# A decoder block's way from its last dense product to its first expert: rewritten, with spare products in it, and the next down weights issued inside the first expert's branch

## The chip, the cores and the metric

The kernel runs on one core of a Trainium2 chip. The metric is device microseconds (us) of one launch; the median of the runs counts. TensorE (PE) does matrix products, PEld are its weight loads, VectorE is DVE, ScalarE is ACT, GpSimd is POOL, and SyncE (SP) issues most transfers.

## The reference, cut to what matters

The block mixes 256 tokens of 2048 channels with two recurrent mixers, projects the mix with `w_out`, and normalises. A router then picks one of 4 groups and 2 of its 8 experts for each token, and each expert's rows go through a gated layer of width 512. All is float32.

```python
x = LN(ALPHA * x + mix @ w_out)                  # 2048 x 2048: the last dense product
lg = x @ w_rg + b_rg                             # 4 groups, top 1
le = x @ w_re + b_re                             # 32 experts, top 2 in the group
for each expert e:                               # 32 experts, rows sorted by expert
    h = silu(xb @ w_gate[e]) * (xb @ w_up[e])    # 2048 -> 512, twice
    out += weight * (h @ w_down[e])              # 512 -> 2048
x = LN(ALPHA * x + out + sigmoid(x @ w_pg) * (p @ w_ple))
```

## The kernel before

The program order is written by hand, engine by engine. The first stage is dense: weights of 512 KB arrive through four staging buffers, ACT and DVE split each into a high and a low part (L217, L218, buffers in `B[6]`, `B[7]`), and PE multiplies (L282, L283, and L290 to L292 in `run`). The last four dense units are `w_out`, 512 output channels each, 16 steps `k` each. In a step PE does three products for each of the two token blocks `tb`. When a unit is done, `evac_out` adds the residual (L916), takes statistics (L932), transposes the rows (L925, copied by L927) and adds to the router's products (`logits`, L906). After the last unit come the normalisation's scale (L1117 to L1123), a second small set of products that puts the router's sums into rows (L1127), and the router itself: a chain of some 25 small DVE operations from L1201 to L1222, products that count and rank the tokens of each expert (`prk`, L1225 to L1229), and the ranks (L1238). A one-hot matrix for the first expert (`hot_quad`, L1343) lets PE pick the expert's rows (`pick`, L1414); they are transposed and scaled (`turn`, L1423 to L1428).

The second stage goes through the experts. An expert's gate and up weights are four quarters of 2 MB (`("gu", e, q)`, order `QS = (2, 1, 0, 3)`), its down weights two halves of 2 MB (`("dn", e, q)`). They live in big buffers B0 to B10; `idle` is the list of free ones, `seq` the order of the weights, and `fetch` gives the next weights of `seq` to the free buffers, on SP's queue. Five of the first ten transfers are placed between the dense weights (`HOOK_W`, numbers of loads counted from the first of `w_out`), the other five follow the last dense product. The residual rows `xres` lie in B9 until then.

For expert `e`, `up_part` multiplies the quarters (L1355, 32 products each), `glu` applies the gate (L1360 to L1362), and an expert that may have more than 32 rows has a branch on its count `c`: with more, a second set of rows is done; otherwise (`Else`) PE picks the next expert's rows (L1414) and transposes the hidden rows (L1366). Then the quarters' buffers are released and refilled, `turn` and the down products follow (`down`, L1376). For expert 0 one of the four buffers becomes the accumulator `acc` (zeroed by POOL, L1685), and the experts are sorted by count after `turn` (`sort`, L1298 to L1310); only then can SP load the weights of experts 2 and later, since their numbers come from the sort.

A wait on PE is a wait on a count that PE's instructions raise. In the program before, the count is raised once, by 64, after the fourth quarter of expert 0. What the other side of the branch would have raised is added by the first product inside `Else`. The buffers' release counts include that, so SP's first two loads after the branch and POOL's zeroing wait for that product.

## Time and profile before

| | |
|---|---|
| three runs | 1820.55 us median, 1819.59 to 1824.2 |
| the profiled execution | 1823.52 us, of them a span of 1821.8 in the profile |
| PE, DVE, ACT busy | 1599.6 us (88%), 794.0 (44%), 607.4 (33%) |
| moved by DMA | 541.38 MB, 297 GB/s over the span |
| experts' transfers on SP | 62 up, 62 gate and 60 down of 2048.0 KB, 4 down of 1024.0 KB, 10 of `w_pg` |

A busy share is an average over two different stages, so the rows to read are those by time: the 40 slices of the span, tables over chosen stretches, and the list of instructions in order of time. A row of that list gives start, duration, engine, line, operation, output from inputs, the count, and in brackets the idle time before it and what ended it. `SPq` rows are issues of transfers; `DMA_DIRECT2D` on L967 is a quarter, on L971 a down half.

### The profile page before, as it was taken

What the parts mean: (1) busy time and instruction counts of PE and PEld (TensorE: products, weight loads), DVE (VectorE), ACT (ScalarE), POOL (GpSimd) and SP (SyncE); (2) the same over time, 40 slices, a digit from 0 to 9 for tenths busy, and PEclk for the clock granted to TensorE, in tenths of its full rate; (3) what the DMA queues carried; (4) which work ended last, traced back from release to release, by engine and by line L of the source; (5) the groups of instructions that cost most, each with busy time, mean ns of one, the idle gap of its engine ahead of it and who ended that gap; (6) DMA issues with size and microseconds to landing.
All of it is one profiled execution on the core that took longest, in us unless ns stands there. A gap on an engine that the chain in (4) does not pass through costs nothing. (4 is left out here: it accounts for less than half of the span.)

```text
span 1821.8 us, 34784 instructions
## 1 busy us (share of the span) xinstructions
PE 1599.6 (88%) x14339; PEld 1081.0 (59%) x14339; DVE 794.0 (44%) x1664; ACT 607.4 (33%) x1179; POOL 26.6 (1%) x38
## 2 busy tenths in 40 slices
PE   7999999999989999997879787897797878987876
PEld 6787787877868778875447444455364433433332
DVE  5675756757765777854331121220211313221206
ACT  5645645646455465544111111111111111111122
POOL 0000000000000000000000000000000000000002
PEclk9999999999999999998899998899899998998888
DMA  7443434434336347975899999999999999999997
GB/s 243 157 153 116 157 129 134 151 117 141 127 105 196 106 139 240 362 228 222 353 426 427 426 425 426 393 425 426 426 426 426 426 426 396 385 427 425 426 426 323
DMA packets 68073, 541.38 MB, mean 297 GB/s; under 512 B 7740, under 2 KB 12108, under 8 KB 42016
## 3 DMA queue, kind: packets, MB, share of 16 engines
q1 hardware_dynamic: 67152, 537.33, 74.4%
q8 instruction: 142, 2.33, 0.5%
q0 software_dynamic: 720, 1.25, 0.3%
q14 instruction: 59, 0.48, 0.1%
HBM read 536.44 MB, written 2.36 MB: 296 GB/s over the span
## 5 line engine op out<-in xcount | busy, mean ns | idle before, releaser
L282 PE MATMUL dps<-B,B 128*128 128x512 f32 x1456 | 538.7, 410 | 12.1 <-ACT B L217 9.3
L283 PE MATMUL dps<-B,B 128*128 128x256 f32 x1456 | 411.0, 282 | 4.8 <-DVE B L218 4.7
L218 DVE TENSOR_TENSOR B<-B,B 128x512 fp32r<-128x512 f32 (+1 forms) x464 | 312.3, 683 | 188.9 <-ACT B L217 184.0
L1355 PE MATMUL dps<-B,B 128*32 128x256 f32 x3968 | 260.6, 418 | 87.9 <-DMA B<-in_w_gate_dram 39.9
L217 ACT ACTIVATE B<-B 128x512 fp32r<-128x512 f32 (+1 forms) x464 | 283.7, 623 | 161.8 <-PE dps L282 62.5
L282 PEld LDWEIGHTS dps<-B,B 128*128 128x128 f32 x1456 | 275.6, 189 | 84.5 <-ACT B L217 11.7
L283 PEld LDWEIGHTS dps<-B,B 128*128 128x128 f32 x1456 | 277.0, 190 | 12.3 <-DVE B L218 10.0
L1355 PEld LDWEIGHTS dps<-B,B 128*32 128x32 f32 x3968 | 139.3, 119 | 214.3 <-DMA B<-in_w_gate_dram 50.8
L1361 DVE SCALAR_TENSOR_TENSOR M<-M,dps 128x128 f32<-128x128 f32 x31 | 8.9, 289 | 401.9 <-ACT M L1360 401.9
L1719 ACT ACTIVATE B<-mps 32x512 f32<-32x512 f32 x120 | 70.6, 588 | 191.4 <-PE mps L1376 190.3
L1376 PE MATMUL mps<-B,M 128*32 128x512 f32 x992 | 127.4, 653 | 5.9 <-issue 2.7
L1170 PE MATMUL mps<-B,B 128*128 128x206 f32 (+1 forms) x640 | 112.8, 337 | 0.6 <-DVE B L1159 0.3
L1360 ACT ACTIVATE M<-dps 128x128 f32<-128x128 f32 x31 | 8.6, 278 | 309.1 <-PE dps L1355 309.1
L1170 PEld LDWEIGHTS mps<-B,B 128*128 128x128 f32 x640 | 110.6, 190 | 1.6 <-DVE B L1159 0.6
L1376 PEld LDWEIGHTS mps<-B,M 128*32 128x32 f32 x992 | 31.5, 118 | 83.5 <-issue 76.9
L290 PE MATMUL dps<-B,B 128*128 128x512 f32 x192 | 76.1, 396 | 2.7 <-ACT B L217 2.7
L292 PE MATMUL dps<-B,B 128*128 128x512 f32 x192 | 75.3, 392 | 0.9 <-DVE B L218 0.8
L291 PE MATMUL dps<-B,B 128*128 128x512 f32 x192 | 74.9, 390 | 0.0
L1427 DVE TENSOR_TENSOR B<-mps,V 128x512 f32<-128x512 f32 x31 | 21.4, 692 | 90.8 <-PE mps L1423 90.8
L1396 PE MATMUL mps<-B 128*128 128x512 f32 (+1 forms) x128 | 56.7, 595 | 0.7 <-ACT B L1719 0.7
L1183 DVE SCALAR_TENSOR_TENSOR C<-C,mps 128x412 f32<-128x412 f32 (+1 forms) x10 | 5.8, 581 | 102.6 <-PE mps L1175 102.6
L1182 ACT ACTIVATE C<-mps 128x412 f32<-128x412 f32 (+1 forms) x10 | 5.1, 512 | 129.9 <-issue 70.4
(465 smaller groups left out, 1585.0 us busy)
## 6 DMA issues: line engine op xcount, KB each, us to landing
B<-in_w_up_dram SPq DMA_DIRECT2D x62, 2048.0 KB, 24.5
B<-in_w_gate_dram SPq DMA_DIRECT2D x62, 2048.0 KB, 21.8
B<-in_w_down_dram SPq DMA_DIRECT2D x60, 2048.0 KB, 22.9
B<-in_w_gt_dram SPq DMA_DIRECT2D x64, 512.0 KB, 3.7
B<-in_w_rkv_dram SPq DMA_DIRECT2D x48, 512.0 KB, 3.9
B<-in_w_pg_dram SPq DMA_DIRECT2D x10, 1854.0 KB, 30.3
B<-in_w_out_dram SPq DMA_DIRECT2D x32, 512.0 KB, 3.7
B<-in_w_qk_dram SPq DMA_DIRECT2D x16, 512.0 KB, 4.0
```

The lines of the kernel that those rows point to most:

```text
L217: act.activation(h, src, AF.Copy)
L218: dve.tensor_tensor(wl[i % 4][:, :w], src, h.bitcast(FT), op=OP.subtract)
L282: mm(pt_[:, c], h[:, w], x.rearrange("p a t -> p (a t)"), start=k == 0, stop=False)
L283: mm(pt_[:, c, :256], l[:, w], x[:, 0], start=False, stop=k == nk - 1)
L290: mm(o, mh[:, ts_], h, start=first, stop=False)
L291: mm(o, ml[:, ts_], h, start=False, stop=False)
L292: mm(o, mh[:, ts_], l, start=False, stop=last)
L1170: mm(pp[:, tb], x1T[0][:, k, tb * 128:tb * 128 + 128], w[:, k, :n], start=k == 0 and tb == 0, stop=k == 15 and tb == 1)
L1355: mm(pu[32 * j:32 * j + 32].rearrange("p (a f) -> p a f", a=2), xs[:, 4 * q + k, :], w[:, :, k, 128 * j:128 * j + 128], start=q == QS[0] a ...
L1376: mm(pd[32 * j:32 * j + 32, :], hT_[:, 32 * c:32 * c + 32], w[:, c % 2, 512 * j:512 * j + 512], start=c == 0, stop=c == 3)
L1396: mm(pz, SWT[p0:p1, tb * 128:tb * 128 + 128], yq[p0:p1, o], start=True, stop=True)
L1719: act.activation(yq[32 * i:32 * i + 32, 512 * j:512 * j + 512], pd[32 * j:32 * j + 32, :], AF.Copy)
```

## The change

It has seven parts. (1) One more weight transfer is placed between the dense weights (six instead of five); the residual is loaded straight into `x1`, so that B9 is free for it. (2) In the last four steps of the last dense unit the products of token block 1 are held back, and a new `close` does them beside the first block's residual, transposes and router products. (3) The router's sums of the first three units are put into rows during the last unit (`so_far`), and the last unit's share is added in rows directly (`rest_of`). (4) Sixteen products of constants, whose result nobody reads, stand between the router's products and the rank products. (5) The rank products are four instead of five, and the first one-hot matrices are computed ahead of the counts. (6) The sort's products move into expert 0's up stage. (7) SP takes part in expert 0's branch, and on both sides of it issues expert 1's two down halves into the buffers of expert 0's first two quarters.

```diff
@@ constants
+SPARE = 16
...
-HOOK_W = (-10, -5, 1, 7, 17)
+HOOK_W = (-15, -10, -5, 1, 7, 17)
@@ run(), products of an "N" unit
+                block(0)
+                if u == len(units) - 1 and k >= 12:
+                    later.append(block)
+                else:
+                    block(1)
+            if last and later:
+                empty(100, True)
+                close(pt_, later)
+            elif last:
...
@@ logits of units 0 to 2; then, new
+    def so_far():
+
+        cmb = _carve(rw, 612, 512)
+        act.activation(cmb, held[0], AF.Copy)
+        plg.append(bank2())
+        for tb in range(2):
+            for i, (o, n) in enumerate(((0, 32), (32, 4))):
+                mm(plg[0][:, tb, o:o + n], cmb[:, 256 * i + 128 * tb:256 * i + 128 * tb + 128],
+                   cst_("eye32", n, 32 - n), start=i == 0, stop=False)
+
+    def close(p_, blocks):
+
+        x1, = xa
+
+        def turn_rows(tb):
+            pz = held[1 + tb]
+            for j in range(4):
+                pe.transpose(pz[:, j * 128:j * 128 + 128], x1[:, tb, (12 + j) * 128:(12 + j) * 128 + 128], ident)
+            act.activation(xrT[:, 12:, tb * 128:tb * 128 + 128], pz.rearrange("p (k t) -> p k t", k=4), AF.Copy)
+
+        def rest_of(tb):
+            for k in range(12, 16):
+                mm(plg[0][:, tb, :36], xrT[:, k, tb * 128:tb * 128 + 128], wrt[:, k, :], start=False, stop=k == 15)
+
+        def stats_of(tb):
+            dve.bn_stats(stats[:, tb, 3], x1[:, tb, 1536:])
+
+        add_rows(3, 0, p_)
+        act.activation(sm[:, 14:15], one_c, AF.Sqrt)
+        for b in blocks[:3]:
+            b(1)
+        turn_rows(0)
+        stats_of(0)
+        blocks[3](1)
+        add_rows(3, 1, p_)
+        rest_of(0)
+        turn_rows(1)
+        stats_of(1)
+        rest_of(1)
...
@@ where the expert weights go
-    idle, at = deque((0, 1, 2, 3, 10, 5, 9, 6, 7, 4)), {}
+    idle, at = deque((9, 0, 1, 2, 3, 10, 6, 5, 7, 4)), {}
...
-    xres = _carve(big(9), 0, 2, 2048)
-    xa.extend((x1, xres))
+    xa.append(x1)
     for tb in range(2):
-        sp.dma_start(xres[:, tb], xp[tb * 128:tb * 128 + 128, :])
+        sp.dma_start(x1[:, tb], xp[tb * 128:tb * 128 + 128, :])
...
@@ router
+    spare = bank()
+    for i in range(SPARE):
+        mm(spare[:, :128], ident, cst_("ones"), start=True, stop=True)
     prk = bank()
...
-    mm(prk[:, :32], cst_("tris"), fe(msel, 0), start=True, stop=True)
-    mm(prk[:, 32:64], cst_("ones"), fe(msel, 0), start=True, stop=False)
-    mm(prk[:, 32:64], cst_("tris"), fe(msel, 1), start=False, stop=True)
+    mm(prk[:, :64], cst_("tris"), msel.rearrange("p s g e -> p (s g e)"), start=True, stop=False)
+    mm(prk[:, 32:64], cst_("ones"), fe(msel, 0), start=False, stop=True)
...
+    hot0 = _carve(M, 0, 2, 128).rearrange("p s (e n) -> p s e n", e=4)
+    for e in range(2):
+        dve.tensor_tensor(hot0[:, :, 2 + e], rnk.rearrange("p s g e -> p s (g e)")[:, :, e:e + 1].to_broadcast([128, 2, 32]),
+                          cst_("io32", 32)[:, None, :].to_broadcast([128, 2, 32]), op=OP.is_equal)
 
     cnt, most = sb.tile([1, 32], I32, name="cnt"), V[0:1, 129:130].bitcast(I32)
...
@@ experts
-    hot_quad(0)
+    def next_down():
+
+        for key, n in early.items():
+            load(key, n)
+
+    early = {("dn", 1, i): at["gu", 0, q] for i, q in enumerate(QS[:2])}
...
-            c = count(e, engines=CE)
+            c = count(e, engines=CE if e else CE + (ENG.SP,))
...
             up_part(e, q, xg[e % 2], pu[:, 0, :256])
+            if e == 0 and q == QS[2]:
+                sort_rows()
+        if e == 0:
+            sort()
         glu(pu[:, 0, :256], hb)
...
                 turn_h(hbo[0])
+                if e == 0:
+                    next_down()
             with few.Else():
+                if e == 0:
+                    next_down()
                 first(nxt, pz)
...
-        release(*(("gu", e, q) for q in QS))
+        release(*(("gu", e, q) for q in (QS if e else QS[2:])))
...
         if e == 0:
+            at.update(early)
...
-        if e:
-            fetch()
+        fetch()
 
         turn(yo_, xg[(e + 1) % 2])
-        if e == 0:
-            sort()
-            fetch()
```

Line numbers of the changed program are higher: its dense products are L291 to L293, `close` has L941 and L946, the spare products are L1267, the rank products L1270 to L1273, `up_part` L1406, `pick` L1465, its quarter loads L1017 and down loads L1021. In the rows below `dps` and `mps` are accumulators, `B_..` big buffers, `R` and `sm` small ones, `C` the constants; an engine's name in brackets is one it waits for.

PE, end of the last dense unit, before: the last step's products, the residual's transposes and the router's products.

```order
L292 MATMUL dps<-B_70,B_6745 128x512 [waits DVE_49]
L290 MATMUL dps<-B_70,B_6745 128x512
L291 MATMUL dps<-B_70,B_6746 128x512
L292 MATMUL dps<-B_70,B_6745 128x512
L925 MATMUL mps<-C,B_7100 128x128 [waits DVE_49]
L925 MATMUL mps<-C,B_7100 128x128
L925 MATMUL mps<-C,B_7100 128x128 [waits DVE_49]
L925 MATMUL mps<-C,B_7100 128x128 x5
L906 MATMUL mps<-B_74,R 32x256 [waits Activation_49]
```

PE, the same place in the changed program, from the last step of the first block to the held-back products of the second:

```order
L291 MATMUL dps<-B_70,B_6747 128x512 [waits Activation_49]
L292 MATMUL dps<-B_70,B_6748 128x512
L293 MATMUL dps<-B_70,B_6747 128x512 [waits DVE_49]
L291 MATMUL dps<-B_70,B_6747 128x512 [waits DVE_49]
L292 MATMUL dps<-B_70,B_6748 128x512
```

and from the end of the third held-back step to the spare products:

```order
L293 MATMUL dps<-B_70,B_6747 128x512
L941 MATMUL mps<-C,B_7102 128x128 x4
L291 MATMUL dps<-B_70,B_6747 128x512
L292 MATMUL dps<-B_70,B_6748 128x512
L293 MATMUL dps<-B_70,B_6747 128x512
L946 MATMUL dps<-R,B_74 128x36 [waits Activation_49]
L946 MATMUL dps<-R,B_74 128x36 x3
L941 MATMUL mps<-C,B_7102 128x128 [waits DVE_49]
L941 MATMUL mps<-C,B_7102 128x128 x3
L946 MATMUL dps<-R,B_74 128x36 [waits Activation_49]
L946 MATMUL dps<-R,B_74 128x36 x3
L1267 MATMUL mps<-C 128x128 [waits PE_49]
```

Three steps of held-back products, one transposing of the first block, and the fourth step now stand between the two blocks' residuals; the first of the held-back products waits for DVE.

SP, from the last load that follows the dense stage, before: `B_7755` is the tenth buffer; the two loads on L971 are expert 1's down halves, L1658 and L1723 are the branch of expert 0 and what follows, L967 is the third load.

```order
L967 DMA B_7755<-in_w_up_dram 128x4096 [waits DMASW1_49,Pool_49]
L1658 UNCONDITIONAL_BRANCH
L971 DMA B_6725<-in_w_down_dram 128x4096 [waits PE_49]
L971 DMA B_6850<-in_w_down_dram 128x4096 [waits PE_49]
L1723 UNCONDITIONAL_BRANCH
L1498 TENSOR_LOAD cnt [waits DVE_49]
L1502 TENSOR_LOAD sm
L988 COMPARE_AND_BRANCH
L967 ISA
L967 DMA B_7001<-in_w_up_dram 128x4096 [waits PE_49]
```

SP, the same place in the changed program, with `L1719` the branch:

```order
L1017 DMA B_7760<-in_w_up_dram 128x4096 [waits DMASW1_49,Pool_49]
L1549 TENSOR_LOAD cnt [waits DVE_49]
L1719 COMPARE_AND_BRANCH
L1729 COMPARE_AND_BRANCH
L1729 UNCONDITIONAL_BRANCH x2
L1021 DMA B_6605<-in_w_down_dram 128x4096 [waits PE_49]
L1021 DMA B_6727<-in_w_down_dram 128x4096 [waits PE_49]
L1719 UNCONDITIONAL_BRANCH
L1021 DMA B_6605<-in_w_down_dram 128x4096 [waits PE_49]
L1021 DMA B_6727<-in_w_down_dram 128x4096 [waits PE_49]
L1719 UNCONDITIONAL_BRANCH
L1549 TENSOR_LOAD cnt [waits DVE_49]
```

The two down loads stand once on each side of the branch, with SP reading the count first. In the built program PE's count is raised by 16 after each quarter of expert 0, and the two loads wait for the counts after the first and the second quarter, which are reached before the branch; the third load (L1017, later in the order) still waits for the product inside `Else` and for the sorted counts.

More of the change, by code (lines that the diff above doesn't have):

```diff
@@ L221, in split @@
             state["split"] += 1
-    mixers, evacs = [], []
+    mixers, evacs, later = [], [], []
     clock = {"wait": 0}
@@ L286, in run, with block @@
                 mh, ml = x[:, 0], x[:, 1]
-                for tb in range(2):
-                    o = pt_[:, tb, :]
-                    ts_ = slice(tb * 128, tb * 128 + 128)
+                def block(tb, mh=mh, ml=ml, h=h, l=l, first=first, last=last, o=pt_):
+                    o, ts_ = o[:, tb, :], slice(tb * 128, tb * 128 + 128)
                     mm(o, mh[:, ts_], h, start=first, stop=False)
@@ L292, in run @@
                     mm(o, mh[:, ts_], l, start=False, stop=last)
-            if last:
+                block(0)
[7 more added lines that the diff above has]
+            elif last:
                 empty(100, True)
@@ L897, in hybrid_block @@
     lnc = _carve(V, _VEC["b_gate"], 2, 16)
-    held = []
+    held, plg = [], []
     def logits(u):
@@ L906, in logits, with add_rows @@
                 mm(held[0][32 * j:32 * j + 32, 256 * i:256 * i + 256], wrt[:, k, 4 * i:4 * i + 32], xrT[:, k, :],
-                   start=u == 0 and i == 0, stop=u == 3 and i == 1)
+                   start=u == 0 and i == 0, stop=u == 2 and i == 1)
+    def add_rows(u, tb, p_):
+        x1, = xa
+        o = slice(512 * u, 512 * u + 512)
+        dve.scalar_tensor_tensor(x1[:, tb, o], x1[:, tb, o], ALPHA, p_[:, tb], op0=OP.mult, op1=OP.add)
+    def so_far():
[7 more added lines that the diff above has]
+    def close(p_, blocks):
+        x1, = xa
+        def turn_rows(tb):
[20 more added lines that the diff above has]
+        rest_of(1)
     def evac_out(u):
         def f(p_):
-            x1, xres = xa
+            x1, = xa
             if u == 0:
@@ L914, in f @@
             for tb in range(2):
-                o = slice(512 * u, 512 * u + 512)
-                dve.scalar_tensor_tensor(x1[:, tb, o], xres[:, tb, o], ALPHA, p_[:, tb], op0=OP.mult,
-                                         op1=OP.add)
-                if u < 3:
-                    dve.bn_stats(stats[:, tb, u], x1[:, tb, o])
+                add_rows(u, tb, p_)
+                dve.bn_stats(stats[:, tb, u], x1[:, tb, 512 * u:512 * u + 512])
                 yield
@@ L928, in f @@
                 yield
-            if u == 3:
-                act.activation(sm[:, 14:15], one_c, AF.Sqrt)
-                for tb in range(2):
-                    dve.bn_stats(stats[:, tb, u], x1[:, tb, o])
             logits(u)
             yield
+            if u == 2:
+                so_far()
         return f
@@ L1114, in hybrid_block @@
     lgt = _carve(M, 0, 2, 36)
-    cmb = _carve(rw, 612, 512)
     for tb in range(2):
@@ L1118, in hybrid_block @@
     act.activation(mv[:, :, 1:2], mv[:, :, 1:2], AF.Sqrt, bias=eps_l)
-    act.activation(cmb, held[0], AF.Copy)
     dve.reciprocal(mv[:, :, 1:2], mv[:, :, 1:2])
@@ L1123, in hybrid_block @@
         dve.scalar_tensor_tensor(lgt[:, tb], wsum, nmu[:, tb], brt, op0=OP.mult, op1=OP.add)
-    plg = bank()
     for tb in range(2):
-        for i, (o, n) in enumerate(((0, 32), (32, 4))):
-            mm(plg[:, 36 * tb + o:36 * tb + o + n], cmb[:, 256 * i + 128 * tb:256 * i + 128 * tb + 128],
-               cst_("eye32", n, 32 - n), start=True, stop=True)
-    for tb in range(2):
-        dve.scalar_tensor_tensor(lgt[:, tb], plg[:, 36 * tb:36 * tb + 36], mv[:, tb, 1:2], lgt[:, tb], op0=OP.mult,
+        dve.scalar_tensor_tensor(lgt[:, tb], plg[0][:, tb, :36], mv[:, tb, 1:2], lgt[:, tb], op0=OP.mult,
                                  op1=OP.add)
@@ L1292, in ranks, with sort_rows @@
         diagonal(ec, cst_("io32", 32))
-    def sort():
+    def sort_rows():
         pz = bank()
@@ L1299, in sort @@
         act.activation(turned, pz[:32, :], AF.Copy)
+    def sort():
         po = bank()
@@ L1630, in rare @@
                 del at[key]
-    hot_quad(0)
+    def next_down():
+        for key, n in early.items():
+            load(key, n)
+    early = {("dn", 1, i): at["gu", 0, q] for i, q in enumerate(QS[:2])}
+    assert list(early) == seq[len(at):len(at) + 2]
     yo = first(0)
```

## The prediction

> **What bounds the kernel.** I read the 40 slices first.
>
> ```profile
> DMA  7443434434336347975899999999999999999997
> GB/s 243 157 153 116 157 129 134 151 117 141 127 105 196 106 139 240 362 228 222 353 426 427 426 425 426 393 425 426 426 426 426 426 426 396 385 427 425 426 426 323
> ```
>
> From the 21st slice the DMA engines are full at 425 to 427 GB/s nearly to the end, but for three slices of 385 to 396: the expert stage is bounded by its bytes. In the slices before they are not, since the free buffers and PE's pace hold them back. So the question is when the transfers become continuous. Tables over short stretches show it (PE, PEld, DVE, ACT, POOL, then granted clock, DMA share, GB/s):
>
> ```profile
> 846.00:848.00 2.00, 1.32 (x8) 0.84 (x8) 2.00 (x4) 0.49 (x2) 0.00 (x0) 1.00 0.89 205
> 870.00:872.00 2.00, 2.00 (x24) 0.96 (x20) 1.73 (x11) 0.00 (x0) 0.00 (x0) 0.50 0.77 324
> 872.00:874.00 2.00, 2.00 (x40) 1.12 (x36) 1.60 (x9) 0.00 (x0) 0.00 (x0) 0.95 0.00 0
> 878.00:880.00 2.00, 1.45 (x15) 0.74 (x8) 0.00 (x0) 0.77 (x2) 2.00 (x1) 1.00 0.78 164
> 878.50:1138.00 259.50, 213.98 (x1965) 131.60 (x1961) 54.34 (x138) 35.89 (x75) 2.85 (x1) 0.93 1.01 424
> ```
>
> Transfers run from about 847 to 871.8, stop, and resume at about 878.55 (164 GB/s in 878 to 880 is 0.77 us of full rate spread over two). The list by time of SP's issues says why:
>
> ```profile
> 845.46 1.87 SPq L967 DMA_DIRECT2D B<-in_w_up_dram  x2
> 847.51 0.84 SPq L967 DMA_DIRECT2D B<-in_w_gate_dram  x2
> 848.45 0.39 SPq L967 DMA_DIRECT2D B<-in_w_up_dram  x1
> 877.73 0.81 SPq L971 DMA_DIRECT2D B<-in_w_down_dram  x2
> 884.17 0.35 SPq L967 DMA_DIRECT2D B<-in_w_up_dram  x1
> 887.85 1.07 SPq L967 DMA_DIRECT2D B<-in_w_gate_dram  x2
> ```
>
> All ten free buffers are filled by five transfers after the dense stage; then SP waits for the first buffer that expert 0 gives back, until 877.73. Everything loaded later is the same in both programs, so the end moves with this resumption, unless a later gap opens or the transfers ahead of it are late.
>
> **The chain to that release.** Rows in order of time, from the last dense product to expert 0's end:
>
> ```profile
> 840.69 0.69 DVE L218 TENSOR_TENSOR B<-B,B 128x512 fp32r<-128x512 f32 x1 [0.67 <-ACT B L217]
> 845.26 0.39 PE L292 MATMUL dps<-B,B 128*128 128x512 f32 x1
> 845.69 1.28 DVE L916 SCALAR_TENSOR_TENSOR B<-B,dps 128x512 f32<-128x512 f32 x2 [4.31 <-PE dps L292]
> 846.43 0.44 PE L925 MATMUL mps<-C,B 128*128 128x128 f32 x2 [0.78 <-DVE B L916]
> 847.50 1.09 ACT L927 ACTIVATE B<-mps 128x512 f32<-128x512 f32 x2 [6.85 <-PE mps L925]
> 850.83 1.05 PE L1127 MATMUL mps<-C,R 128*128 128x32 f32 x8 [1.13 <-ACT R L1119]
> 852.37 0.16 DVE L1201 TENSOR_REDUCE M<-M 128x2 f32<-128x8 f32 x1
> 856.79 0.61 PE L1225 MATMUL mps<-sm,C 128*128 128x32 f32 x2 [4.91 <-DVE M L1235]
> 859.15 0.22 DVE L1238 SCALAR_TENSOR_TENSOR rnk<-sm,mps 128x64 f32<-128x64 f32 x1 [2.35 <-PE mps L1229]
> 860.06 0.34 DVE L1343 TENSOR_TENSOR M<-rnk,C 128x64 f32<-128x64 f32 x2
> 860.41 3.64 PE L1414 MATMUL mps<-B,M 128*32 128x512 f32 x16 [1.30 <-DVE M L1343]
> 867.41 9.45 PE L1355 MATMUL dps<-B,B 128*32 128x256 f32 x128 [1.51 <-DVE B L1428]
> 876.68 1.89 PE L1414 MATMUL dps<-B,M 128*32 128x512 f32 x16
> 877.84 3.51 POOL L1685 MEMSET B<- 128x4096 f32 x1 [315.99 <-PE dps L1414]
> 880.80 0.69 DVE L1428 TENSOR_TENSOR B<-B,V 128x512 f32<-128x512 f32 x1
> 881.15 1.07 PE L1302 MATMUL mps<-B 32*128 32x32 f32 x8 [0.68 <-ACT B L1299]
> 882.36 5.34 PE L1376 MATMUL mps<-B,M 128*32 128x512 f32 x32
> 888.64 7.11 PE L1355 MATMUL dps<-B,B 128*32 128x256 f32 x128 [0.94 <-PEq L1723]
> ```
>
> Note that POOL at 877.84 and SP at 877.73 are let go by L1414, PE's first product inside the branch, 10.3 us after the quarters were begun. And half the chain ran on a slow clock (column before the DMA share):
>
> ```profile
> 854.50:855.00 0.50, 0.00 (x0) 0.00 (x0) 0.40 (x4) 0.50 (x2) 0.00 (x0) 1.00 1.15 492
> 855.00:855.50 0.50, 0.00 (x0) 0.00 (x0) 0.43 (x3) 0.50 (x2) 0.00 (x0) 0.62 0.99 426
> 872.00:872.50 0.50, 0.50 (x12) 0.28 (x8) 0.43 (x3) 0.00 (x0) 0.00 (x0) 0.82 0.00 0
> 872.50:873.00 0.50, 0.50 (x16) 0.24 (x8) 0.43 (x4) 0.00 (x0) 0.00 (x0) 1.00 0.00 0
> ```
>
> The granted clock is 1.00 to about 855.1 and, after some 17 us at 0.50, 1.00 again from about 872.2 (0.62 and 0.82 are half-microseconds in which it changes). PE had done nothing from 851.9 to 856.8.
>
> **The sum, step by step.** The sum is made on the profiled execution (1823.52 us), which lies 2.97 above the median; I take the difference from the median.
>
> (a) Last dense product to router. Before: 845.65 (845.26 + 0.39) to 852.37, 6.72 us. Now, against the same origin: `so_far` stands in PE's stream during the last unit, 1.05 (L1127's row). The first held-back product waits for the residual of block 0: half of 1.28, plus two handoffs of 0.04 and 0.10, 0.78 in which PE is idle. Four transposes before the last step: 0.44 for two says at most 0.9, I take 0.55. The dense products end at 848.03. Then the residual of block 1, 0.68, beside `rest_of(0)` (eight instructions as L1127: 1.05, to 849.1), four transposes (849.65), a copy (half of 1.09 and a handoff, 850.25), `rest_of(1)` (851.3), and the two closing DVE operations, 0.5 as between L1127's end and 852.37. The router begins at 851.8: 0.6 earlier. Statistics and the square root run beside this. The table load that stood in the way of ACT is issued during the held-back products.
>
> (b) Router to the rank products: 852.37 to 856.79 is all DVE, unchanged. The spare products stand there, on an idle PE; sixteen are 32 instructions, which the trace doesn't show in this form. By L1127 (0.13 each) they last 4.2 us and end at 855.5, in front of the rank products at 856.2: no cost. By L1225 to L1238, on half the clock (0.24 each), they last 7.5 and hang over by 2.6. I take the first, since the clock is still full where they begin.
>
> (c) Rank products: 10 instructions took 2.36 (856.79 to 859.15) at half clock; now eight, at full clock as L1302's eight: 1.07. Saves 1.3. One-hot ahead of the counts: 859.15 to 860.41 is 1.26, now 0.22 + 0.34 and a handoff, 0.64. Saves 0.6.
>
> (d) Pick and turn: 860.41 to 867.41 is 7.00; the same work at full clock is 876.68 to 881.49 (880.80 + 0.69), 4.81. Saves 2.2.
>
> (e) Release: 867.41 to 877.73 is 10.32. Now the first half waits for the first quarter: a quarter of expert 1's 7.11 at full clock is 1.78, with a handoff 1.9. Saves 8.4. SP is free by then: it needs the count, which DVE writes right after the one-hot.
>
> Sum: 0.6 + 1.3 + 0.6 + 2.2 + 8.4 = 13.1 us; the release comes at 864.6, data at 865.4.
>
> **What else is asked of the transfers.** 2048 KB are 2.097 MB, at 424 GB/s 4.95 us. Four instead of five follow the dense stage. The first goes into the staging buffer `B[6]` and waits for DVE's last split, which ended at 841.38 (840.69 + 0.69) and now ends 1.05 later, so it runs from about 843 on, in time that was empty. The other three follow at 848.1 and end near 863. They don't delay 864.6; if they did, the gain would stop near 14.5. The extra transfer in the dense stage lies where PE is full and DMA is not (a share of 0.58):
>
> ```profile
> 680.00:700.00 20.00, 20.00 (x115) 17.33 (x114) 13.87 (x23) 10.81 (x18) 0.00 (x0) 1.00 0.58 185
> ```
>
> I take 0, at most 1.
>
> Behind the release three transfers last 14.85 us, to 880.3. The third needs the sorted counts; before, SP issued it at 884.17, 1.8 after the sort's products ended at 882.36, now by about 873, in time for 875.3. The fourth needs expert 0's down products done. Those ended at 887.7 (882.36 + 5.34), 20.3 after the quarters began, with 5.6 us to spare on transfers that lasted to 893.4. Now: quarters 7.1, the sort's four transposes 0.55 and products 1.2 (881.15 to 882.36), pick 1.9, hidden rows and turn 1.5 (878.57 to the operation before 880.80), down at full clock 3.8 (twice L1414's 1.89): 16.1 after 862.7, so 878.8. The spare time shrinks to 1.5 us; no gap, but little cover. From there compute is 8.9 earlier and the bytes 13.1, so PE must give 4.2 us of waiting. It had them:
>
> ```profile
> 911.57 1.93 PE L1355 MATMUL dps<-B,B 128*32 128x256 f32 x32 [0.57 <-DMA B<-in_w_up_dram]
> 936.06 1.93 PE L1355 MATMUL dps<-B,B 128*32 128x256 f32 x32 [1.13 <-DMA B<-in_w_gate_dram]
> 940.94 3.35 PE L1355 MATMUL dps<-B,B 128*32 128x256 f32 x32 [2.95 <-DMA B<-in_w_up_dram]
> ```
>
> The bracketed waits on DMA are 0.57, 1.13 and 2.95, 4.65 in three of the first quarters. After that the whole stage moves with the bytes. POOL's zeroing keeps its place after the branch and ends long before the first accumulation. Predicted: 1820.55 - 13.1 = 1807.5.
>
> **The clock, and what the skill says.** The row: full until 855.1, 3.2 us after PE's last product, and full again 4.8 us after the quarters began. The Trainium skill, TensorE: Matmul & The Clock Gate, section "What's actually happening", says that a free-running window of about 3.4 us decides, one idle window to slow, one busy to recover; the trace agrees, since 855.1 and 872.2 are five such windows apart. By that rule the spare products, if they last about as long as a window, would keep the clock; an estimate by the page's 1.2 and 2.4 GHz would give 3.4 us for them. Its Part 4 adds that transposes don't count as busy, which speaks against this change: between 848 and 851.3 it has little but transposes and narrow products. No row here tells transposes apart.
>
> **Rivals.** Clock lost all the same: a window falls into 848 to 851.3, the spare products run slowly and hang over into the rank products, or the clock falls behind them. Place: L1267 to L1406. Price: 0.8 in (c) (eight at 0.24), 2.2 in (d), and 0.6 in (e) (a quarter of 9.45 less 1.78), 3.6 in all, with up to 2.6 of overhang: gain 7 to 9.5, 1812. For it: PE is lightly loaded there. Against it: before, 846 to 851.9 was as light and the clock held.
>
> The feed: expert 0's down is later than 878.8 (the sort's products stand ahead of it and wait for DVE's ranks), the 1.5 us are gone and a gap of 1 to 3 opens: gain 10 to 12, 1809.5.
>
> The release isn't earlier, since SP is held at the branch: only (a) to (d) count, 4.7: 1815.9, no measurable change. Against it: SP's count is there some 6 us ahead.
>
> Slower: the sixth transfer between dense weights pushes `w_bm`'s 512 KB loads back, PE starves. A stall of 4.95 once would leave 8 of gain; it decides only from 18.6, nearly four such delays. PE's 20.00 of 20 beside a DMA share of 0.58 speaks against it.
>
> **How the numbers follow.** Likeliest 0.58 (own range 1805 to 1810); clock 0.20; feed 0.13; no earlier release 0.06; slower 0.03. Less than 0.3% (5.5 us) can't be told from no change here. Faster takes in the first three, 0.91; the fourth is same, 0.06; slower 0.03. The range runs from the back-to-back limit, with 2 us of scatter, 1804, to the clock's 1813.5.
>
> **What would show it.** Right: SP's first down load near 864.6, no idle stretch over 2 us in the transfers after 848, clock 1.00 from 848 to the quarters, router from 851.8. Wrong: the clock at 0.50 in the rank products or the pick (b, d), the load at the quarters' end (e), transfers idle near 880 (feed), PE waiting on `w_bm` near 700.

## The result, and the profile after

The changed kernel took 1813.77 us (median of five, 1810.76 to 1814.93) beside 1820.70 of the kernel before (five, 1819.59 to 1824.20); the ratio over the rounds is 0.9947 (0.9934 to 0.9960). Timed a second time, beside runs of the kernel before of its own (e5 below), it was 1813.01 beside 1824.55, ratio 0.9941 (0.9928 to 0.9953). So it is faster, by 9.6 us (7.3 to 12.0) by the first ratio and 10.8 (8.6 to 13.1) by the second; 13.1 was predicted. The medians as they stand differ by 6.9 us the first time, just outside the first interval, and by 11.5 the second, so the size is less certain than the direction. The first median lies 0.3 above the range's upper end.

The page of the profiled execution (1814.93 us):

```profile
span 1813.3 us, 34848 instructions
GB/s 240 162 152 117 158 118 137 152 118 134 132 105 186 116 126 283 340 252 210 392 427 426 426 426 426 397 426 424 427 427 426 426 427 382 381 425 426 424 427 335
```

The 20th slice moves more (392 GB/s, 353 before), and two of the three late dips are deeper (397, 382 and 381 against 393, 396 and 385).

To compare executions I need an origin that the change doesn't touch. SP's last issue of a dense weight (`w_out`) is one: it comes before the first held-back product. Its row gives start and length of a group of issues; the last issue is at their sum. Of the kernel before, and then SP's list of the changed kernel:

```profile
820.20 9.42 SPq L204 DMA_DIRECT2D B<-in_w_out_dram  x4
```

```profile
820.67 12.14 SPq L205 DMA_DIRECT2D B<-in_w_out_dram  x5
845.52 0.33 SPq L1017 DMA_DIRECT2D B<-in_w_up_dram  x1
868.18 2.05 SPq L1021 DMA_DIRECT2D B<-in_w_down_dram  x2
876.74 0.35 SPq L1017 DMA_DIRECT2D B<-in_w_up_dram  x1
882.24 0.94 SPq L1017 DMA_DIRECT2D B<-in_w_gate_dram  x2
894.12 0.33 SPq L1017 DMA_DIRECT2D B<-in_w_up_dram  x1
```

The last dense issue was at 829.62 before and at 832.81 now, 3.19 later. Nothing that the change does explains that: it was there well ahead of the sixth transfer, which SP issues at 697.74, in the first weights of `w_o` and `w_bm` (before, then now):

```profile
568.16 31.82 SPq L204 DMA_DIRECT2D B<-in_w_o_dram  x11
690.23 11.63 SPq L204 DMA_DIRECT2D B<-in_w_bm_dram  x5
571.82 28.42 SPq L205 DMA_DIRECT2D B<-in_w_o_dram  x10
693.86 3.84 SPq L205 DMA_DIRECT2D B<-in_w_bm_dram  x2
697.74 0.42 SPq L1017 DMA_DIRECT2D B<-in_w_up_dram  x1
```

3.66 and 3.63 later there, 3.19 at the end. The first down load (the release) is 48.11 after it before and 35.37 now: 12.74 earlier. The span less that origin is 992.18 before and 980.49 now: 11.69 shorter. Over the executions below, the last dense issue lies between 829.62 and 832.28 in the five of kernels built on the one before, and between 828.54 and 832.81 in the nine built on the changed one; the means are 830.55 and 830.90. So the 3 us are scatter of that stage, and a cost of the sixth transfer isn't seen in it: the means differ by 0.35, and PE was busy 20.00 of 20 us from 680 to 700 and from 700 to 720 in both kernels.

The chain, by the rows that answer to those of before:

```profile
847.83 0.50 PE L291 MATMUL dps<-B,B 128*128 128x512 f32 x1 [0.78 <-DVE B L922]
854.44 5.44 PE L1267 MATMUL mps<-C 128*128 128x128 f32 x32
855.10 0.16 DVE L1243 TENSOR_REDUCE M<-M 128x2 f32<-128x8 f32 x1
859.72 0.33 PE L1270 MATMUL mps<-sm,C 128*128 128x64 f32 x2
861.36 1.92 PE L1465 MATMUL mps<-B,M 128*32 128x512 f32 x16 [0.67 <-ACT M L1277]
866.18 5.39 PE L1406 MATMUL dps<-B,B 128*32 128x256 f32 x96 [1.51 <-DVE B L1479]
883.03 1.89 PE L1406 MATMUL dps<-B,B 128*32 128x256 f32 x26 [0.94 <-PEq L1785]
885.95 5.81 PE L1406 MATMUL dps<-B,B 128*32 128x256 f32 x102 [1.03 <-issue]
```

The first held-back product waits 0.78, as predicted. The router (L1243) starts 22.29 after the origin, 22.75 before. The pick (L1465) starts 28.55 after it, 30.79 before; from pick to quarters it is 4.82, before 7.00; from quarters to release 2.00, before 10.32. The clock fell once, beneath the spare products (the column before the DMA share; edges worked out from the half-microseconds in which it changes, 854.98 and 858.39; a slow stretch of this length, 3.41 us, is called a window of the clock in what follows):

```profile
854.50:855.00 0.50, 0.50 (x6) 0.50 (x6) 0.36 (x3) 0.50 (x2) 0.00 (x0) 0.98 0.61 262
855.00:855.50 0.50, 0.50 (x5) 0.50 (x4) 0.40 (x4) 0.50 (x1) 0.00 (x0) 0.50 1.15 492
858.00:858.50 0.50, 0.50 (x5) 0.50 (x5) 0.42 (x3) 0.50 (x2) 0.00 (x0) 0.61 1.23 524
858.50:859.00 0.50, 0.50 (x7) 0.50 (x6) 0.41 (x3) 0.50 (x1) 0.00 (x0) 1.00 1.00 426
```

The transfers pause briefly around the release and thin out once more behind it (last columns: DMA share, GB/s):

```profile
868.00:870.00 2.00, 2.00 (x44) 1.23 (x40) 1.76 (x12) 0.00 (x0) 0.00 (x0) 1.00 0.63 127
894.00:896.00 2.00, 1.47 (x15) 0.44 (x8) 0.00 (x0) 0.77 (x2) 0.00 (x0) 1.00 0.91 258
896.00:898.00 2.00, 2.00 (x20) 0.75 (x22) 1.46 (x3) 0.00 (x0) 0.00 (x0) 1.00 0.89 369
```

Against 426, the last two rows lack 1.06 us. They belong to expert 2's last quarter, issued at 894.12, when the gates issued at 882.24 had run out.

### The profile page after: what moved, and what is told of

The parts are those of the page before. It is cut to its first block, busy times and chain, and to the rows that moved or that the text cites. A ratio compares the mean times of both kernels' runs of the same rounds, so it can differ in the third digit from the quotient of the medians.

```text
span 1813.3 us, 34848 instructions
## 1 busy us (share of the span) xinstructions
PE 1599.5 (88%) x14369; PEld 1090.8 (60%) x14369; DVE 794.1 (44%) x1664; ACT 607.5 (34%) x1179; POOL 26.5 (1%) x38
## 3 DMA queue, kind: packets, MB, share of 16 engines
q0 software_dynamic: 720, 1.25, 0.3%
## 5 line engine op out<-in xcount | busy, mean ns | idle before, releaser
L1406 PE MATMUL dps<-B,B 128*32 128x256 f32 x3968 | 255.3, 413 | 86.1 <-DMA B<-in_w_up_dram 43.1
L283 PEld LDWEIGHTS dps<-B,B 128*128 128x128 f32 x1456 | 276.0, 190 | 85.1 <-ACT B L218 11.5
L284 PEld LDWEIGHTS dps<-B,B 128*128 128x128 f32 x1456 | 277.5, 191 | 11.7 <-DVE B L219 9.4
L1406 PEld LDWEIGHTS dps<-B,B 128*32 128x32 f32 x3968 | 139.8, 118 | 204.1 <-DMA B<-in_w_up_dram 47.4
L1427 PE MATMUL mps<-B,M 128*32 128x512 f32 x992 | 122.3, 631 | 10.9 <-PEq L1654 6.6
L291 PE MATMUL dps<-B,B 128*128 128x512 f32 x192 | 77.4, 403 | 3.1 <-ACT B L218 2.3
L293 PE MATMUL dps<-B,B 128*128 128x512 f32 x192 | 76.3, 397 | 0.3
```

The lines of the kernel that those rows point to most:

```text
L283: mm(pt_[:, c], h[:, w], x.rearrange("p a t -> p (a t)"), start=k == 0, stop=False)
L284: mm(pt_[:, c, :256], l[:, w], x[:, 0], start=False, stop=k == nk - 1)
L291: mm(o, mh[:, ts_], h, start=first, stop=False)
L293: mm(o, mh[:, ts_], l, start=False, stop=last)
L1406: mm(pu[32 * j:32 * j + 32].rearrange("p (a f) -> p a f", a=2), xs[:, 4 * q + k, :], w[:, :, k, 128 * j:128 * j + 128], start=q == QS[0] a ...
L1427: mm(pd[32 * j:32 * j + 32, :], hT_[:, 32 * c:32 * c + 32], w[:, c % 2, 512 * j:512 * j + 512], start=c == 0, stop=c == 3)
```

## The experiments

All were timed in rounds beside the kernel before. "Release" is SP's first load of `w_down` less its last dense issue, and "end" the span less that issue, both of one profiled execution and as differences from the kernel before (48.11 and 992.18); "timed" is the ratio, with its interval, and the microseconds that it makes of the median of before beside it (1820.7 to 1824.6).

| kernel | release | end | timed |
|---|---|---|---|
| changed | -12.7 | -11.7 | 0.9947 (0.9934 to 0.9960), -9.6 |
| changed again (e5) | -12.7 | -12.2 | 0.9941 (0.9928 to 0.9953), -10.8 |
| e1 release as before | -3.2 | -3.2 | 0.9977 (0.9966 to 0.9988), -4.2 |
| e2 release alone | -6.6 | -2.4 | 0.9970 (0.9958 to 0.9983), -5.5 |
| e3 no spare products | -10.4 | -10.4 | 0.9958 (0.9944 to 0.9972), -7.7 |
| e4 five prefetches | -12.7 | -13.3 | 0.9933 (0.9916 to 0.9950), -12.2 |
| e6 dense tail as before | -12.3 | -9.5 | 0.9940 (0.9928 to 0.9952), -10.9 |
| e7 sort as before | -9.8 | -9.2 | 0.9957 (0.9944 to 0.9970), -7.8 |
| e8 second release early | -11.8 | -10.6 | 0.9956 (0.9943 to 0.9968), -8.0 |
| e9 spare products alone | -5.4 | -5.3 | 0.9979 (0.9969 to 0.9990), -3.8 |
| e10 release and sort | -6.6 | -5.2 | 0.9965 (0.9952 to 0.9978), -6.4 |
| e11 more spare products | -12.9 | -9.2 | 0.9960 (0.9946 to 0.9975), -7.3 |
| e12 without the dense part | -7.6 | -5.7 | 0.9959 (0.9946 to 0.9973), -7.5 |

### Does the end follow the release? (e1, e2)

e1 undoes one part of the change:

```
-            c = count(e, engines=CE if e else CE + (ENG.SP,))
+            c = count(e, engines=CE)
...
-                if e == 0:
-                    next_down()          # in both sides of the branch
...
-        release(*(("gu", e, q) for q in (QS if e else QS[2:])))
+        release(*(("gu", e, q) for q in QS))
```

> The changed kernel, with expert 1's down loads issued after expert 0's branch again, as before. If the bytes set the end, SP's first down load comes at about 877 instead of 868.2 (10.3 after the quarters begin at 866.2, plus the sort's products now in front), the stretch without transfers grows from under 1 us to about 8, the small gaps near 870 and 895 (about 1 us together) go, and the time is 7 to 8 us above the changed kernel's: 0 to 3 us faster than the kernel before. If PE's chain sets the end and the transfers only follow, the time stays within 1 us of the changed kernel's (7 to 10 faster than before).

```profile
874.86 0.81 SPq L1021 DMA_DIRECT2D B<-in_w_down_dram  x2
```

The load comes 44.89 after the last dense issue (829.97), 9.5 after the changed kernel's, and the end moves with it: -3.2 and -3.2. The time is 5.4 to 6.6 us above the changed kernel's two, a little less than the 7 to 8 expected. The first theory holds. What is left, 4.2 timed, is terms (a) to (d): the quarters started at 863.16, 4.6 earlier than before (33.19 after the last dense issue against 37.79), and 1.7 went again on a slow window in them (96 instructions took 7.07 instead of 5.39).

e2 is the kernel before with that part alone:

```
...
+            c = count(e, engines=CE if e else CE + (ENG.SP,))
...
+                if e == 0:
+                    next_down()          # in both sides of the branch
...
-        release(*(("gu", e, q) for q in QS))
+        release(*(("gu", e, q) for q in (QS if e else QS[2:])))
```

> The kernel before with one part of the change: expert 1's two down loads are issued inside expert 0's branch, half of the gate and up buffers released first. If the release alone carries the 8.4 us of the prediction's term (e), the time falls by about 8. If it is worth only what the transfers ahead leave, SP issues at about 869.3 while five transfers run to 871.8; the two down transfers then end at 881.7, the next one still waits for the sorted counts (884.2), a new gap of about 3.3 opens, and of the 6.75 us without transfers about 3.4 are gained: 3 to 4 us faster than before.

```profile
871.63 3.05 SPq L971 DMA_DIRECT2D B<-in_w_down_dram  x2
884.86 0.35 SPq L967 DMA_DIRECT2D B<-in_w_up_dram  x1
882.00:884.00 2.00, 1.97 (x20) 1.39 (x24) 0.99 (x7) 0.00 (x0) 0.24 (x1) 1.00 0.62 262
884.00:886.00 2.00, 2.00 (x24) 0.65 (x20) 1.20 (x8) 0.00 (x0) 0.00 (x0) 1.00 0.54 119
886.00:888.00 2.00, 0.99 (x16) 0.14 (x8) 0.00 (x0) 1.04 (x2) 0.00 (x0) 1.00 0.72 229
```

The release is 6.6 earlier, the end 2.4. The third load still waits for the sorted counts, at 884.86 (+0.2 against before), and the transfers fall to 262, 119 and 229 GB/s, 3.1 us without bytes: the second theory, by the trace. The timing, -5.5 (-3.1 to -7.7), doesn't tell the two apart.

### What stands ahead of the release and behind it (e4, e10, e12)

e4 is the changed kernel with five hooks instead of six:

```
-HOOK_W = (-15, -10, -5, 1, 7, 17)
+HOOK_W = (-10, -5, 1, 7, 17)
```

> The changed kernel without the sixth transfer inside the dense stage (five as before, so five follow it). If the sixth costs nothing in the dense stage, the last dense issue comes no earlier than in the changed kernel by more than the scatter of runs, the transfers ahead run to about 872 behind loads issued at 868.2, the resumption is 2.9 later and the 1 us of later gaps goes: about 2 us slower than the changed kernel. If the sixth delays the dense weights by about 3 us, which is where the gain's missing part would then have gone, the dense stage ends 3 earlier and the time is about 1 us below the changed kernel's.

```profile
832.45 12.99 SPq L1017 DMA_DIRECT2D B<-in_w_up_dram  x2
```

Both theories were wrong in one point. The sixth transfer, no longer hooked in, isn't put behind the dense stage: a buffer is there for it (`B[10]`, since one of the five went into `B[9]`, free because the residual is now added in place), so SP issues it at 832.45, at once after the last dense load (832.40), into time that was empty; only the second of this row, 13 us later, waits. Release and time are the changed kernel's. So the sixth hook as such brings nothing; that the free buffer matters instead is an inference, to which e12 adds.

e10 is e2 with the sort at expert 0's quarters as well:

```
...
             up_part(e, q, xg[e % 2], pu[:, 0, :256])
+            if e == 0 and q == QS[2]:
+                sort_rows()
+        if e == 0:
+            sort()
         glu(pu[:, 0, :256], hb)
...
-        if e:
-            fetch()
+        fetch()
         turn(yo_, xg[(e + 1) % 2])
-        if e == 0:
-            sort()
-            fetch()
```

> The kernel before with two parts: the down loads issued in the branch, and the sort inside the quarters. The release alone brought SP's load 6.6 forward against the last dense split, but by the trace only 2 to 3 us of the end, for the third transfer waited for the sorted counts (its issue moved by +0.2). If that wait was what cost it, the third load now comes near 880, ahead of the two down transfers' end, and 2 to 3 us more are gained: the end 4.5 to 5.5 earlier than before by the trace. If the gap only moves to the next transfer (expert 2's gates, which need expert 0's down product), the end gains less than 1 over the release alone.

```profile
882.83 0.35 SPq L967 DMA_DIRECT2D B<-in_w_up_dram  x1
```

Against the last dense issue (832.28) the third load is 4.0 earlier than before, and the end 5.2 earlier instead of 2.4. By the trace, the wait for the sorted counts was what e2 lost; the timings, -6.4 and -5.5, overlap.

e12 is e10 with the spare products. It lacks the new dense tail, the residual in place and the sixth transfer:

```
+    spare = bank()
+    for i in range(SPARE):               # SPARE = 16
+        mm(spare[:, :128], ident, cst_("ones"), start=True, stop=True)
     prk = bank()
```

> The kernel before with three parts: spare products, down loads in the branch, sort inside the quarters. Left out are the new end of the dense stage, the residual added in place (which gives a buffer back early) and the sixth transfer: five transfers still follow the dense stage. The release should come 23 us after the last dense split as SP issues it (24.1 with the later split of the kernel before), 12 earlier than before. If the release sets the end, the trace's end lies 10 to 11 earlier than before against the split. If the five transfers do, which run to 29.4 after the split whatever PE does, it lies 5.5 to 6.8 earlier: then 4 to 5 us of the whole change come from the buffer given back early, which the prediction took as given and priced at nothing.

```profile
871.26 2.83 SPq L972 DMA_DIRECT2D B<-in_w_down_dram  x2
870.00:872.00 2.00, 2.00 (x24) 0.94 (x20) 1.76 (x11) 0.00 (x0) 0.00 (x0) 0.50 0.97 410
872.00:874.00 2.00, 2.00 (x40) 0.99 (x36) 1.72 (x10) 0.00 (x0) 0.00 (x0) 0.85 1.02 348
```

Here four windows of the clock were lost in spite of the spare products, and the release is only 7.6 earlier. Yet the transfers hardly paused: they ran full to 872 and at 348 in 872 to 874, so the five ahead ended just as the loads came, and an earlier release had only some 0.4 us left to gain in these rows. The end is 5.7 earlier, in the 5.5 to 6.8 that the five transfers allow. That doesn't separate the two limits, since the release and the transfers came due together. e9 alone gives 5.3 and e10 5.2; together they give 5.7, not 10.5, and the changed kernel, with the buffer given back early besides, 11.7 to 12.2. By the timings, 3.8 and 6.4 alone, 7.5 (4.9 to 9.8) together, 9.6 to 10.8 changed, neither the missing part of the sum nor the distance to the changed kernel is clear of the intervals. e12's profiled execution was the slowest of its five (1818.94, median 1815.30), so the 6 us between its end and the changed kernel's are rather too many.

### The clock and the spare products (e3, e9, e11)

e3 is the changed kernel without them:

```
-SPARE = 16
+SPARE = 0
```

> The changed kernel without the sixteen spare products (SPARE = 0). If they keep the clock, the clock is 0.50 from about 855 until some 5 us into the quarters, the rank products take 0.8 longer, pick and turn 2.2, the first quarter 0.6; SP's first down load comes 3.3 to 3.6 later, and the time is about 3.4 above the changed kernel's. If they are of no use, since the clock was at 0.50 for 3.4 us beneath them anyway and would recover in the same way without them, the time is within 0.5 us of the changed kernel's and the load comes 0.3 earlier.

```profile
855.20 0.66 PE L1270 MATMUL mps<-sm,C 128*128 128x64 f32 x2 [4.86 <-issue]
857.75 3.64 PE L1465 MATMUL mps<-B,M 128*32 128x512 f32 x16 [0.66 <-DVE M L1287]
866.28 2.05 SPq L1021 DMA_DIRECT2D B<-in_w_down_dram  x2
```

Rank products and pick ran on half the clock (0.66 and 3.64 against 0.33 and 1.92), the release is 2.4 later than the changed kernel's, the time 1.9 to 3.1 above, with overlapping intervals. The first quarter was at full clock again, so its 0.6 fell away. The first theory, a third smaller. The profiled execution was the quickest of this kernel's six (1811.90, median 1816.26), so its end says little.

e9 is the kernel before with the sixteen spare products, the lines that e12 adds to e10.

> The kernel before with the sixteen spare products alone, in the place they have in the changed kernel. Before, the clock was 0.50 in five windows of 3.41 us, from 12.7 us after the last dense split to 4.8 us into the quarters. If the spare products keep it there, the rank products take 1.1 less, pick and turn 2.2, the quarters up to the first product in the branch 2.3: SP's first down load comes 5.6 earlier, five transfers ahead end just then, nothing opens behind, and the time is 5 to 5.6 us below the kernel before's. If the windows still fall to 0.50 later, since PE idles between pick and turn, only 1 to 2 us are gained.

```profile
872.66 1.28 SPq L972 DMA_DIRECT2D B<-in_w_down_dram  x2
864.67 7.11 PE L1359 MATMUL dps<-B,B 128*32 128x256 f32 x128 [1.51 <-DVE B L1432]
```

Release 5.4 and end 5.3 earlier (5.6 and 5 to 5.6 expected), with the quarters at full clock; timed 3.8 (1.8 to 5.7). Three lines of spare work give by the trace nearly half of what the whole change does, by the timing 35 to 40%.

e11 puts nine more into the changed kernel (`more(n)` issues n products like the spare ones into a PSUM bank of its own):

```
     yo = first(0)
+    more(3)
     turn(yo, xg[0])
+    more(6)
```

> The changed kernel with three spare products more behind expert 0's pick and six behind its turn, where PE waits for ACT and DVE. Of six executions of kernels with sixteen spare products, three lost a window of the clock in pick or in expert 1's quarters (0.9 to 2.9 us of the release), three lost it beneath the spare products, where it costs 0.3. If idle PE between pick and quarters is what decides those windows, none falls between 857 and 872 (counted with the last dense split at 844), SP's load stays 22.4 to 22.8 after the split, and the time is 0 to 1 below the changed kernel's. If the spare products are too few, or stand in front of the turn's transposes, a slow window remains there or the load comes later than 23.

```profile
863.37 5.39 PE L1406 MATMUL dps<-B,B 128*32 128x256 f32 x96 [0.17 <-DVE B L1479]
875.57 3.64 PE L1465 MATMUL dps<-B,M 128*32 128x512 f32 x16 [3.20 <-issue]
865.37 2.06 SPq L1021 DMA_DIRECT2D B<-in_w_down_dram  x2
```

(The windows meant by "expert 1's quarters" fell in expert 0's, as in e1.) No window was lost up to 873.8 and the release is the earliest of all, 35.20 after the last dense issue. But then PE stood 3.20 us in front of the branch's first product, with a mark for "waited for nothing that the profile shows"; two windows were lost, the third load came 3.4 later than the changed kernel's, and the time is 2 to 4 above. In this one execution the clock held up to the branch; a better kernel it isn't.

### The dense tail, the sort, the second release (e5 to e8)

e5 is the changed kernel, timed again.

> The changed kernel itself, timed again. If the missing part of the predicted 13.1 us is mostly scatter of code that the change doesn't touch (the profiled executions so far put the last dense split anywhere from 840.5 to 845.5, without order between kernels), the time comes out 10 to 12 us below the kernel before's of the same chip: 0.6 for the small gaps in the transfers and 0.5 to 1 in the release subtracted from 13.1. If the change costs the dense stage about 3 us, it comes out 7 to 8 below, as between the first medians, and the last dense split lies at 844 or later again. The release comes 22.7 after the last dense split in both cases.

10.8 below, and the last dense issue at 831.31: the first theory. Release 35.37 after it, the same to a hundredth.

e6 brings the old end of the dense stage back:

```
-                if u == len(units) - 1 and k >= 12:
+                if False:                # nothing held back, no close()
...
-            if u == 2:
-                so_far()                 # the copy and the products against eye32 come after the last unit again
...
```

> The changed kernel with the old end of the dense stage: no products held back, the router's logits all after the last step, its bias sums turned afterwards. By term (a) the router begins 0.5 later against the last dense split once 1.05 is allowed for the split's own move (release some 24.2 after the split instead of 22.7), and the time is 0.5 above the changed kernel's, which can't be told. If the rewritten tail is worth more than that (the clock, or ACT's table load that it takes out of the chain), the release comes 26 or more after the split and the time 2 or more above.

```profile
820.33 12.14 SPq L205 DMA_DIRECT2D B<-in_w_out_dram  x5
868.33 2.06 SPq L1024 DMA_DIRECT2D B<-in_w_down_dram  x2
```

35.86 after 832.47, 0.49 later than the changed kernel's; the ratio is the same. Term (a) is that small. (This execution lost 2 us more behind the release; I haven't traced where.)

e7 puts the sort behind the branch again:

```
-            if e == 0 and q == QS[2]:
-                sort_rows()
-        if e == 0:
-            sort()
...
         turn(yo_, xg[(e + 1) % 2])
+        if e == 0:
+            sort_rows()
+            sort()
+            fetch()
```

> The changed kernel with the sort behind expert 0's branch again. SP's third load behind the release (expert 2's first, which needs the sorted counts) then comes about 13 after the release instead of 8.6, the two down transfers end at 10.7, and a gap of about 3 opens; the later gap of about 1.1 before expert 2's last quarter closes. If the transfers set the end, the time is about 1.8 above the changed kernel's. If the later work can take the gap up, it is the same within 0.5.

The third load came 12.65 after the release, as expected, and the transfers fell to 98 and 168 GB/s in 878 to 882. But two windows of the clock were lost as well, the release was 2.9 later, and from release to end this execution is no longer than the changed kernel's (944.7 us against 945.1). So the gap is shown, its price isn't: the timed 2 to 3 us above the changed kernel hold both.

e8 issues expert 1's successors early too:

```
+        if e == 1:
+            release(*(("gu", e, q) for q in QS))
+            fetch()
         glu(pu[:, 0, :256], hb)
...
```

> The changed kernel with one thing more: expert 1's gate and up buffers are released, and the next loads issued, ahead of its branch, each after its own quarter. If the shortfall of transfers 26 to 30 us after the release (258 and 369 GB/s, 1.1 us lost) is this release being late, SP issues expert 2's last quarter some 8 us earlier, the transfers run on there at 425 GB/s, and the time is 1.1 below the changed kernel's. If something else takes its place (SP or PE held by the extra signals, or the end set by other work), the time is within 0.5 of it or above.

```profile
894.00:896.00 2.00, 1.82 (x16) 0.50 (x16) 0.43 (x4) 0.00 (x0) 0.00 (x0) 1.00 0.98 418
896.00:898.00 2.00, 1.47 (x17) 0.78 (x17) 0.41 (x1) 0.77 (x2) 0.00 (x0) 1.00 1.05 430
1130.00:1200.00 70.00, 58.24 (x651) 27.45 (x655) 19.89 (x49) 9.57 (x21) 0.00 (x0) 0.93 0.95 399
1130.00:1200.00 70.00, 59.77 (x631) 27.19 (x623) 19.74 (x49) 9.56 (x21) 0.00 (x0) 0.88 0.97 407
```

The gap closed (418 and 430 GB/s), but the time didn't fall: 2 us above the changed kernel's, the intervals overlapping. 0.9 of it is a window lost in expert 0's quarters, ahead of the release. Most of the rest was given back at 1130 to 1200 (third row e8, fourth the changed kernel's second execution): 399 and 407 GB/s over 70 us are 4.5 and 3.2 us without bytes. As I read it, the transfers wait there for buffers that PE holds, and bytes that came 1 us sooner only wait longer; what PE does in that stretch I haven't followed.

## Why the prediction was right and where it was wrong

**Right in kind, and in the chain.** The end moves with the release (e1, e9): from release to end the fourteen executions took 943.5 to 945.9 us, but for e6 (946.9), e11 (947.8) and e2 (948.3). The release came 12.7 earlier where 13.1 was worked out. By terms: (a) 0.46 (0.6 predicted); rank products and one-hot 1.78 (1.9), of which the spare products took back some 0.2 (the rank products began 26.91 after the origin; in e11, where the spare products took 3.82, 26.67); (d) 2.18 (2.2); (e) 8.32 (8.4). e1 and e6 confirm (e) and (a) by undoing them.

**Term (b), the spare products at nothing.** They took 5.44, between the 4.2 and the 7.5, since one window of 3.41 us fell on them. The choice of the lower end was wrong in size and harmless. The reason given, "since the clock is still full where they begin", isn't safe: where the window falls differs by execution, and in e12 four were lost after them.

**The feed: the step that failed.** "From there compute is 8.9 earlier and the bytes 13.1, so PE must give 4.2 us of waiting. It had them": the waits I quoted are at 911 to 941. The transfer that ran dry hung on expert 1's branch, at 894, and expert 1's quarters had no wait for data before to give (their row at 888.64 says PEq, 0.94). Its load before:

```profile
898.12 0.33 SPq L967 DMA_DIRECT2D B<-in_w_up_dram  x1
```

That is 68.50 after the last dense issue, and 61.31 now (894.12): 7.2 earlier, where the bytes were 12.7 earlier. What had to cover the difference were the five transfers between the release and this load, 24.75 us at 4.95 each: before, it came 20.39 after the release, now 25.94. Compute was as worked out as far as the start of expert 1's quarters, 8.8 earlier. There PE stopped once, 1.03 us for nothing that the profile shows, and the quarters lasted 8.73 us instead of 7.11; the prediction has no term for such a stop. In e3 they ran without one:

```profile
881.14 7.11 PE L1406 MATMUL dps<-B,B 128*32 128x256 f32 x128 [0.94 <-PEq L1785]
```

Its load came 24.45 after its release, and from 20 to 60 us after the release it moved 426 GB/s, the changed kernel 416 and 415. That is one execution, and why PE stopped stays open. The fourth transfer, which I had watched, was in time. The gap is 1.06, at the lower end of that rival's 1 to 3, and the whole from release to end is 0.6 to 1.1 longer than before in two executions.

**Given back late.** One more place was not in the sum. At 1490 to 1570 the kernel before lacks 7.5 us of bytes (386 GB/s over 80 us) and the changed one 9.6 and 9.2 (375, 377). One reason shows in the last quarter of an expert there, before and after:

```profile
1495.52 1.93 PE L1355 MATMUL dps<-B,B 128*32 128x256 f32 x32 [1.62 <-DMA B<-in_w_up_dram]
1486.35 3.61 PE L1406 MATMUL dps<-B,B 128*32 128x256 f32 x32 [2.96 <-DMA B<-in_w_up_dram]
```

PE waits 2.96 instead of 1.62, and the quarter runs at half the clock, 1.7 longer. That isn't the whole of it: in e5 the quarter was as slow (3.42) after a wait of 1.25, e4 lacks 9.0 with this quarter at full clock, and e1, whose release is only 3.2 earlier, lacks 9.4.

**What I priced at nothing.** "Four instead of five follow the dense stage" was taken as given. The transfers ahead ran out in these microseconds, before and now (last columns: DMA share, GB/s):

```profile
871.00:872.00 1.00, 1.00 (x16) 0.42 (x12) 0.86 (x5) 0.00 (x0) 0.00 (x0) 0.50 0.67 270
867.00:868.00 1.00, 1.00 (x28) 0.58 (x20) 0.90 (x8) 0.00 (x0) 0.00 (x0) 1.00 0.35 148
```

So the five ended at about 871.6, 42.0 after the last dense issue, and the four at about 867.4, 34.5 after it; 863, or 33.4, was worked out. With five, the data of a release at 35.4 would have waited some 6 us for them. This is read from the rows: e12 fits it, but there the clock held the release back to just that time, and no run has the buffer alone.

**The base.** Of the 5.9 us between 1807.5 and the mean of the two medians, 1813.4, about 3 come from the base. I took the three runs' median, 1820.55, and treated the profiled execution, 1823.52, as 2.97 too long. Beside the experiments the kernel before has medians of 1823.53, 1824.55, 1823.17 and 1823.77 (23, 11, 18 and 9 runs): the profiled execution was the typical one. (In the first round itself the kernel before had 1820.70, the base I took; by the medians of that round alone all of the miss lies in the gain.) The other 3 are the gain, 10.2 (mean of the two ratios' 9.6 and 10.8) instead of 13.1: 0.4 of the release, 0.6 to 1 of the feed, and some 1.5 that the traces' ends (-11.7 and -12.2) don't show; the intervals of the timing cover that.

**The rivals.** Clock lost: in its full form (3.6) it didn't happen in the changed kernel's two executions, whose one window fell on the spare products and cost some 0.2; in part it did in e1, e7 and e8. No earlier release: refuted. Sixth transfer starving PE: not seen (e4, and PE's 20.00 of 20 above). Feed: it happened, on another load than the one I named and for another reason.

## What to carry to other kernels

When two things must both be there before a stream of transfers can go on (the transfers ahead done, a buffer free), shortening either alone gives only the distance to the other: price the parts together, and ask of each what then ends last. Follow the shift load by load until it settles, since each load hangs on its own release; a wait that PE has 20 to 50 us later doesn't help the load that is due now; the transfers already issued ahead of it do. And judge differences of 0.3% from an origin just ahead of the change, not from spans or from a median of three.

## What the runs showed of the hardware

The clock goes slow in whole steps. The slow stretches around the release lasted 3.41 us (changed kernel, e1, e4, e5, e6, e8, e9, and three times in e7), 6.83 (e11), 10.24 (e3), 13.66 (e12), 17.06 (before, e10) and 20.48 (e2): one to six times 3.41. Their place against the work differs between kernels and executions, so that the same 32 instructions took 3.82 us in e1, e7, e8, e11 and e12 and 5.44 or 5.45 in the changed kernel's two, e4, e6 and e9. The Trainium skill, TensorE: Matmul & The Clock Gate, "What's actually happening", gives 3413 ns for a free-running window; the trace agrees.

PE stops in the code behind a branch for nothing that the profile shows: 1.03 us within expert 1's quarters in the changed kernel, 0.32 to 1.57 in eight other executions of kernels with the spare products (all but e7), none in the four without them (before, e2, e3, e10). In e11 it also stopped for 3.20 in front of the branch's first product. So part of what the spare products win may be given back there; no run settles it. The Trainium skill, Runtime: NRT & Kernel Launch, "Instruction fetch mechanics", says that a taken branch to code that isn't loaded has to wait for its fetch by DMA; no run here shows whether that is the cause.
